# Seven mixer projections and half of an embedding gate as joint blocks with seven-product pairs in an fp32 encoder layer

## The chip, the core and the metric

One core of one Trainium2 chip. The time is device microseconds of one execution. Every matmul is 128x128 by 128x512, in fp32r. To reach fp32 accuracy, each fp32 product is made as three matmuls: every operand is split into a rounded part (hi) and a remainder (lo), and lo·hi, hi·hi and hi·lo are summed in PSUM.

## The reference

256 tokens, 2048 features, weights in fp32 that are each used once. Cut to what matters here:

```
h = h + 1/2 * SwiGLU_1(RMSNorm(h))                # 2048 -> 5632 -> 2048
u = RMSNorm(h); z = u @ W_in                      # columns: NA q|k|v (1024 each), q-latent 512,
                                                  # kv-latent 512, rope key 64, gate_A 2048, gate_B 2048
A  = NeighbourhoodAttention2D(q, k, v) @ W_branch_A      # 8 heads, with a table of biases
Bm = MLA(q-latent, kv-latent, rope key) @ W_branch_B     # 8 heads, through W_uq and W_ukv
h = h + (sigmoid(gate_A) * A + sigmoid(gate_B) * Bm) @ W_out
h = h + 1/2 * SwiGLU_2(RMSNorm(h))
h = h + sigmoid(RMSNorm(h) @ W_pl_gate) * (p @ W_pl)     # per-layer embedding
out = RMSNorm(h)
```

## The kernel before, in words

**Stream of granules.** The main loop (line 1160 on) walks a list of granules, each a step. A granule has a conversion and its matmuls. The conversion (`conv`) starts the load of raw weights on SyncE's queue into one of three raw tiles R, and then `split` (L89) makes hi on ScalarE (the cast L90) and lo on VectorE (the subtraction L91) into tiles W0 to W5. `convert()` runs ahead in the list for as long as W tags are free; a tag comes back when its granule's matmuls are done. All engines keep the order in which the program issues: in each step first the conversions that have tags, then the granule's matmuls (`triple`, L95 to L97), then the step's tasks. `at(d, fn)` puts a task d steps later. Tasks are evacuations' second halves, transposes, attention and sums of squares.

**Plain units.** `unit` computes 256 tokens by 512 columns; with K row tiles of 128 that is 6K matmuls (96 for K = 16), in granules of two row tiles (12 matmuls, one W tag out of W0 to W3). Its sums stand in two of PSUM banks 0 to 3; side work (`bank()`) takes banks 4 to 7. The stationary operand is x transposed, split into hi and lo, the moving one the weights.

**Joint blocks.** `Block` computes two such 512-column products at once over pairs of row tiles, so each pair is a 2x2 by 2x2 block product. A plain pair (`Plain`) needs 8 products of three matmuls, 24. Pairs 2, 4 and 6 (`SEVEN`) use seven products of sums of the operands, 21 matmuls, issued as `SevenA` (9) and `SevenB` (12). They need sums of weights on VectorE (L258 to L261) and a "form" of x with eight tiles (`sums` on VectorE, L358, and a second split). A pair takes two W tags out of six, so two pairs lie converted ahead of the one in use. The products accumulate in all eight banks: plain pairs use banks 4, 5, 7 and 3; SevenA begins bank 0; SevenB begins banks 6, 2 and 1 in this order among its products. At the block's end VectorE combines the eight sums in eight additions, `early` (L192 to L195) and `late` (L201 to L204), and `done` takes the four results. While a block runs, side work has only those of banks 0 to 2 that its products have not begun.

**Forms.** `make_form` transposes four 128x128 tiles of h (or of a product) into one bank, scales it on ScalarE by the norm's gain, and takes lo on VectorE. For a seven-product pair it first writes a scratch tile Z on ScalarE, makes sums there on VectorE, and one step later splits Z into hi and lo.

**Where joint blocks are used.** In both SwiGLUs: 11 chunks of gate and up (the first chunk of the layer excepted), and the down products, in three parts, two blocks each. All of the mixer and the embedding is plain units: three latents and the rope key, W_ukv and W_uq, NA q, k, v, gate_B, then for each of four column groups gate_A, branch A and branch B, then W_out. MLA attention runs as tasks beside the NA projections (a head pair every five granules), NA attention beside the gate_B units. When the last down block of a SwiGLU is done, `added` adds its results to h on VectorE (L549) and `new_xT` transposes, scales and splits the new x (L332, L336, L344) for the plain units behind it; sums of squares follow four to six steps later. The table of NA biases is loaded by 16 DMAs on POOL's queue (L822) while the NA projections run, and POOL masks it with eight `affine_select`s (L827, L829). `na_qk_evac` scales a result on VectorE (L840) and transposes it one step later (L847).

## Time and profile before

| | |
|---|---|
| median of 3 runs | 2152.14 us (2151.56 to 2153.6) |
| the profiled execution | 2156.39 us, its span 2154.7 us |
| mean granted TensorE clock in it | 0.997 |
| largest groups | L91 on VectorE 1066.4 us in 697 operations, L90 on ScalarE 911.5 us in 697 |
| loads of weights | 408.46 MB on SyncE's queue, 57.2% of the DMA engines' span |

The lines of the trace are in us from the span's start. A timeline row has start, length, engine, line, operation, what it writes and reads, a count, and in brackets the idle time before it and what ended that. A windows row has the stretch, its length, and for each of PE, PEld, DVE, ACT and POOL the busy us and instructions, then the mean granted clock, the DMA share and GB/s. Matmul records are longer than their spacing, since matmuls overlap.

### The profile page before, as it was taken

To read this page: it belongs to the slowest core of one execution; us is meant where nothing else is said; L and a number is where in the kernel's file an instruction comes from. 1 tells how busy PE (TensorE), PEld (TensorE's weight loads), DVE (VectorE), ACT (ScalarE), POOL (GpSimd) and SP (SyncE) were. 2 spreads that over 40 slices of the span, in tenths; PEclk is the share of its full clock that TensorE was granted. 3 is DMA by queue.
4 is the path that set the end of the run, shared out by engine and by line. 5 is a ranking of instruction groups with operands and counts; after the bars stand their busy time and mean duration, and the time that the engine had idled before them with its cause. 6 is when DMAs were issued, how large, how long until landed. Compare 5 with 4: busy or idle time off the path is not lost.

```text
span 2154.7 us, 25398 instructions
## 1 busy us (share of the span) xinstructions
PE 2138.3 (99%) x9693; PEld 1774.8 (82%) x9693; DVE 1716.2 (80%) x1856; ACT 1137.0 (53%) x1172; POOL 62.9 (3%) x73
## 2 busy tenths in 40 slices
PE   9999999999999999999999999999999999999997
PEld 8888888888888888878888888888888888888886
DVE  6899889998999855555655556999989998899975
ACT  7455555554555554435544445555545555555553
POOL 0000100000000000230000000000000000000000
PEclk9999999999999999999999999999999999999999
DMA  7555766667565554565455556466676657765653
GB/s 262 189 195 196 238 196 205 202 212 236 196 205 185 169 194 138 158 192 176 144 189 195 187 185 207 164 197 202 218 228 205 205 191 215 220 209 184 220 197 127
DMA packets 218026, 421.99 MB, mean 196 GB/s; under 512 B 13576, under 2 KB 14160, under 8 KB 217776
## 3 DMA queue, kind: packets, MB, share of 16 engines
q1 hardware_dynamic: 212048, 408.46, 57.2%
q0 software_dynamic: 5824, 11.89, 3.2%
q8 instruction: 76, 1.25, 0.2%
q14 instruction: 46, 0.38, 0.0%
q10 hardware_dynamic: 32, 0.01, 0.0%
HBM read 409.83 MB, written 2.10 MB: 191 GB/s over the span
## 4 chain that ended last, share of the span: by engine, by line
PE 97%; DVE 1%; DMA 1%; ACT 0%; issue 0%; POOL 0%; DVEq 0%; ACTq 0%; POOLq 0%
PE B L97 31%; PE B L95 31%; PE B L96 31%; PE B L368 1%; DMA R<-in_w_in_dram 1%; PE B L776 1%; PE B L344 0%; DVE W L91 0%; PE B L762 0%; PE B L800 0%; PE B L883 0%; PE B L801 0%; ACT W L90 0%; PE B L847 0%; PE B L1121 0%
## 5 line engine op out<-in xcount | busy, mean ns | idle before, releaser
L91 DVE TENSOR_TENSOR W<-R,W 128x1024 fp32r<-128x1024 f32 (+2 forms) x697 | 1066.4, 1548 | 318.4 <-ACT W L90 315.9
L90 ACT CAST W<-R 128x1024 fp32r<-128x1024 f32 (+2 forms) x697 | 911.5, 1311 | 722.6 <-DVE R L258 290.3
L95 PE MATMUL B<-W,X 128*128 128x512 f32 x2113 | 832.8, 394 | 0.0
L97 PE MATMUL B<-W,X 128*128 128x512 f32 x2113 | 823.9, 390 | 0.5 <-DVE W L91 0.5
L96 PE MATMUL B<-W,X 128*128 128x512 f32 x2113 | 823.1, 390 | 0.0
L97 PEld LDWEIGHTS B<-W,X 128*128 128x128 f32 x2113 | 397.1, 188 | 84.7 <-DVE W L91 1.1
L96 PEld LDWEIGHTS B<-W,X 128*128 128x128 f32 x2113 | 397.4, 188 | 80.8
L95 PEld LDWEIGHTS B<-W,X 128*128 128x128 f32 x2113 | 397.4, 188 | 80.7
L95 PE MATMUL B<-W,H 128*128 128x512 f32 x800 | 312.6, 391 | 0.2 <-DVE X L336 0.2
L97 PE MATMUL B<-W,H 128*128 128x512 f32 x800 | 311.6, 390 | 0.3 <-DVE W L91 0.3
L96 PE MATMUL B<-W,H 128*128 128x512 f32 x800 | 311.3, 389 | 0.0
L97 PEld LDWEIGHTS B<-W,H 128*128 128x128 f32 x800 | 150.2, 188 | 32.2 <-DVE W L91 1.1
L95 PEld LDWEIGHTS B<-W,H 128*128 128x128 f32 x800 | 150.2, 188 | 31.5 <-issue 0.8
L96 PEld LDWEIGHTS B<-W,H 128*128 128x128 f32 x800 | 150.2, 188 | 30.8
L258 DVE TENSOR_TENSOR R<-R 128x1024 f32<-128x1024 f32 x95 | 116.4, 1225 | 3.3
L261 DVE TENSOR_TENSOR R<-R 128x512 f32<-128x512 f32 x95 | 65.8, 693 | 3.2
L260 DVE TENSOR_TENSOR R<-R 128x512 f32<-128x512 f32 x95 | 65.7, 692 | 3.3
L386 ACT CAST H<-B 128x512 fp32r<-128x512 f32 x28 | 15.9, 588 | 90.5 <-PE B L368 90.5
L551 POOL DMA_DIRECT2D h<-t x16 | 14.1, 1018 | 1409.3 <-DVE t L201 1189.6
L538 ACT ACTIVATE s<-t,sm 128x512 f32<-128x512 f32 x42 | 28.1, 717 | 31.9 <-DVE t L201 31.9
L539 DVE SCALAR_TENSOR_TENSOR pt<-pt,sm,s 128x512 f32<-128x512 f32 x42 | 29.5, 744 | 0.0
L332 ACT ACTIVATE X<-B,gT 128x256 fp32r<-128x256 f32 x40 | 15.7, 478 | 25.3 <-PE B L344 25.3
(207 smaller groups left out, 1024.5 us busy)
## 6 DMA issues: line engine op xcount, KB each, us to landing
R<-in_ffn_w_down_dram SPq DMA_DIRECT2D x176, 512.0 KB, 5.2
R<-in_ffn_w_gate_dram SPq DMA_DIRECT2D x170, 512.0 KB, 3.7
R<-in_ffn_w_up_dram SPq DMA_DIRECT2D x168, 512.0 KB, 4.7
R<-in_w_in_dram SPq DMA_DIRECT2D x64, 1024.0 KB, 5.2
R<-in_w_out_dram SPq DMA_DIRECT2D x16, 1024.0 KB, 5.0
R<-in_w_pl_gate_dram SPq DMA_DIRECT2D x16, 1024.0 KB, 5.1
R<-in_w_branch_a_dram SPq DMA_DIRECT2D x8, 1024.0 KB, 4.9
R<-in_w_branch_b_dram SPq DMA_DIRECT2D x8, 1024.0 KB, 4.9
```

The lines of the kernel that those rows point to most:

```text
L90: S.copy(hi, r)
L91: V.tensor_tensor(out=lo, in0=r, in1=hi.bitcast(F32), op=ALU.subtract)
L95: PE.matmul(o, xl, hi, start=start, stop=False)
L96: PE.matmul(o, xh, hi, start=False, stop=False)
L97: PE.matmul(o, xh, lo, start=False, stop=stop)
L258: V.tensor_tensor(out=raw[:, 0:4:3, :], in0=raw[:, 0:3:2, :], in1=raw[:, 3:4, :].to_broadcast([P, 2, 512]), op=ALU.add)
L260: V.tensor_tensor(out=raw[:, 2, :], in0=raw[:, 0, :], in1=raw[:, 2, :], op=ALU.add)
L261: V.tensor_tensor(out=raw[:, 1, :], in0=raw[:, 2, :], in1=raw[:, 1, :], op=ALU.add)
L368: PE.transpose(ps[:, j * P:j * P + P], src(t, 2 * i + k), ident)
L538: S.activation(s[t], g, AF.Silu, scale=r[:, t:t + 1])
L539: V.scalar_tensor_tensor(out=u, in0=u, scalar=rh[:, t:t + 1], in1=s[t], op0=ALU.mult, op1=ALU.mult)
L776: PE.matmul(b[:, j * T:j * T + T], vsl(heads[j], kt), pts[j][:, kt, :], start=(kt == 0), stop=(kt == 1))
```

## The change

Joint blocks take the place of plain units for: kv-latent with q-latent, NA v, the second half of gate_B, gate_A (two blocks), W_out (two blocks), and the first half of the embedding gate. The order of units changes: latents, NA q (first half), rope key, W_ukv, W_uq, rest of q, k, v; branch B, gate_B, gate_A, branch A, W_out. x is held in forms throughout (`first_tile` reads plain tiles from them), so `new_xT` goes and `added` calls `new_forms` after both blocks: forms of the first 512 columns one step, of the second two steps later, sums of squares at steps five and six. All seven-product forms of h share the scratch tag Z; a pending split is flushed before Z is taken again. `bank()` inside a block gives out banks 0, 1, 2, 1, 2 in this order from its start. MLA and NA attention run a head pair every four granules, beside plain units only, and hold W4 and W5 meanwhile (`hold`, `loose`). The bias load moves to one step after the v block, and VectorE masks it eight steps later by adding a window tile. NA's output is kept in fp32 and split once at the end. The core of the diff:

```diff
     def bank():
+        if seven_on[0]:
+            turn["block"] += 1
+            return psum_tile((0, 1, 2, 1, 2)[turn["block"] - 1])
         turn["side"] += 1
-        if seven_on[0]:
-            return psum_tile((1, 2, 0)[turn["side"] % 3])
         return psum_tile(4 + turn["side"] % 4)
...
+    pending = []
+
+    def flush():
+        while pending:
+            pending.pop()()
+
-    def make_form(where, i, j, src, gc=None):
+    def make_form(where, i, j, src, gc=None, full=False, scratch="Z"):
...
-        z = piece("Z", [P, 8, P])
+        flush()
+        z = piece(scratch, [P, 8, P])
+        c = 0 if full else 1
         scaled(z[:, 0:4, :].rearrange("p a b -> p (a b)"), ps, gc)
         sums(z[:, 0:4, :], z[:, 4:8, :])
-        at(1, lambda: split(f[:, 0, 1:8], f[:, 1, 1:8], z[:, 1:8, :]))
+        pending.append(lambda: split(f[:, 0, c:8], f[:, 1, c:8], z[:, c:8, :]))
+        at(1, flush)
         return f
...
+    def added(n, nxt, full=True):
+
+        def done(c11, c12, c21, c22):
+            for k, t, o in ((n, 0, c11), (n, 1, c21), (n + 1, 0, c12), (n + 1, 1, c22)):
+                hs = h[:, t, k * 512:k * 512 + 512]
+                if nxt:
+                    V.tensor_tensor(out=hs, in0=hs, in1=o, op=ALU.add)
+                else:
+                    G.dma_start(hs, o, accum_op=ALU.add)
+            if nxt:
+                for k in range(2):
+                    at(1 + k, lambda k=k: new_forms(n + k, nxt, full))
+                    next_stat(nxt, n + k, 5 + k)
+        return done
...
-                if n == 0:
-                    at(1, lambda: new_xT(0, nxt))
-                    at(1, lambda: new_xT(1, nxt, (0,)))
-                    at(2, lambda: new_xT(1, nxt, (1,)))
-                    next_stat(nxt, 0, 5)
-                    next_stat(nxt, 1, 6)
-                else:
-                    at(2, lambda: new_xT(2, nxt))
-                    at(3, lambda: new_xT(3, nxt))
-                    next_stat(nxt, 2, 4)
-                    next_stat(nxt, 3, 5)
...
+        def latents(c11, c12, c21, c22):
...
+            for d, (which, place, z) in enumerate((("kva", "H0", (c11, c21)), ("qa", "H2", (c12, c22)))):
+                for t in range(2):
+                    V.tensor_scalar(out=z[t], in0=z[t], scalar1=r[:, t:t + 1], scalar2=None, op0=ALU.mult)
+                at(1 + 2 * d, lambda which=which, place=place, z=z: tr(which, place, z))
...
+            def masked():
+                for t in range(2):
+                    q = M["bias"][t].rearrange("p a i c -> p (a i) c")
+                    V.tensor_tensor(out=q, in0=q, in1=window[:, None, :].to_broadcast([P, 32, 64]), op=ALU.add)
+            at(9, masked)
+            at(1, bias)
...
+        joint(wi, 3584, 3072, x, latents)
+        plain(0, na_qk_evac("nq", 0, "H1"))
+        unit(rows(wi, 4096, 64), 16, 64, narrow_x, kr_evac)
         for u in range(4):
             unit(rows(w_ukv[0], u * 512), 4, 512, lop("kva"), ukv_evac(u))
         for u in range(3):
             unit(rows(w_uq[0], u * 512), 4, 512, lop("qa"), uq_evac(u))
+        plain(512, na_qk_evac("nq", 1, "H1"))
         for u in range(2):
+            plain(1024 + u * 512, na_qk_evac("nk", u, "H3"))
+        joint(wi, 2048, 2560, x, values)
         for n in range(4):
+            unit(rows(w_branch_b[0], n * 512), 8, 512, oop("ob"), yb_evac(n))
+        for n in range(2):
+            plain(6208 + n * 512, gb_evac(n))
+        joint(wi, 6208 + 1024, 6208 + 1536, x, gb_done(2))
+        for n in (0, 2):
+            joint(wi, 4160 + n * 512, 4160 + n * 512 + 512, x, ga_done(n))
         for n in range(4):
             unit(rows(w_branch_a[0], n * 512), 8, 512, oop("oa"), ya_evac(n))
+        for n in (0, 2):
+            joint(w_out[0], n * 512, n * 512 + 512, form_of(mixed), added(n, "ffn2", False))
...
+        wg, wp = w_pl_gate[0], w_pl[0]
+        Block([rows(wg, 0), rows(wg, 512)], form_of(forms), 8, gates)
+        unit(rows(wp, 0), 2, 512, pop, pl_evac(0))
+        unit(rows(wp, 512), 2, 512, pop, pl_evac(1))
+        unit(rows(wg, 1024), 16, 512, None, gate_evac(2), xtile=first_tile)
...
-    tasks.setdefault(first_pl + 4, []).append(E["ptr"])
+    tasks.setdefault(first_pl + 1, []).append(lambda: at(1, E["ptr"]))
```

`E["ptr"]` transposes the embedding's input p into one bank and splits it (ScalarE, then VectorE).

## The prediction

> **What bounds the kernel now.** I read the page first: busy shares, then the chain that ended last.

> ```profile
> span 2154.7 us, 25398 instructions
> PE 2138.3 (99%) x9693; PEld 1774.8 (82%) x9693; DVE 1716.2 (80%) x1856; ACT 1137.0 (53%) x1172; POOL 62.9 (3%) x73
> ...
> PE 97%; DVE 1%; DMA 1%; ACT 0%; issue 0%; POOL 0%; DVEq 0%; ACTq 0%; POOLq 0%
> ```

> The chain is TensorE almost from end to end, so the time is the number of matmuls times their spacing, plus the places where TensorE waits. The windows view gives the spacing, for a joint gate-and-up block and the joint down block behind it:

> ```profile
> 428.99:471.36 42.37, 42.37 (x193) 35.17 (x192) 39.78 (x40) 24.05 (x22) 0.00 (x0) 1.00 0.60 199
> 471.36:512.84 41.48, 41.48 (x185) 34.35 (x184) 36.13 (x32) 20.84 (x17) 3.48 (x4) 1.00 0.75 230
> ```

> The second has no transposes. By the listing a joint block of eight pairs is 5 x 24 + 3 x 21 = 183 matmuls: 41.48 / 183 = 0.2267 us each, with no wait. The first has eight transposes more: 0.89 us, 0.11 each. But VectorE is busy 39.78 of 42.37 us there: joint blocks run at TensorE's pace with little to spare.

> The timelines of one block start show how little. It is the last down block of the first SwiGLU, which already hands on to the mixer with additions into h and transposed forms. TensorE:

> ```profile
> 677.60 0.39 PE L95 MATMUL B<-W,H 128*128 128x512 f32 x1
> ...
> 689.59 0.39 PE L97 MATMUL B<-W,H 128*128 128x512 f32 x1
> 689.83 0.60 PE L344 MATMUL B<-ident,h 128*128 128x128 f32 x4
> ...
> 692.81 0.39 PE L97 MATMUL B<-W,H 128*128 128x512 f32 x1
> 693.44 0.47 PE L95 MATMUL B<-W,H 128*128 128x512 f32 x1 [0.25 <-DVE X L336]
> ...
> 695.60 0.39 PE L95 MATMUL B<-W,H 128*128 128x512 f32 x1
> ...
> 696.06 0.39 PE L97 MATMUL B<-W,H 128*128 128x512 f32 x1
> ```

> VectorE, then ScalarE:

> ```profile
> 678.22 0.68 DVE L204 TENSOR_TENSOR pt<-B,pt 128x512 f32<-128x512 f32 x1
> 678.82 2.28 DVE L91 TENSOR_TENSOR W<-R,W 128x2048 fp32r<-128x2048 f32 x1
> 681.01 1.29 DVE L549 TENSOR_TENSOR h<-h,t 128x512 f32<-128x512 f32 x2
> ...
> 683.42 1.75 DVE L91 TENSOR_TENSOR W<-R,W 128x1536 fp32r<-128x1536 f32 x1
> 685.21 1.23 DVE L258 TENSOR_TENSOR R<-R 128x1024 f32<-128x1024 f32 x1
> ...
> 687.80 2.44 DVE L336 SCALAR_TENSOR_TENSOR X<-B,gT,X 128x256 fp32r<-128x256 f32 x6
> 690.16 2.35 DVE L91 TENSOR_TENSOR W<-R,W 128x1024 fp32r<-128x1024 f32 x2
> 692.42 0.87 DVE L336 SCALAR_TENSOR_TENSOR X<-B,gT,X 128x256 fp32r<-128x256 f32 x2
> 693.21 3.95 DVE L91 TENSOR_TENSOR W<-R,W 128x2048 fp32r<-128x2048 f32 x2
> ```

> ```profile
> 690.46 0.84 ACT L332 ACTIVATE X<-B,gT 128x256 fp32r<-128x256 f32 x2 [1.49 <-PE B L344]
> ...
> 699.91 1.05 ACT L90 CAST W<-R 128x1024 fp32r<-128x1024 f32 x1 [0.32 <-DVE R L261]
> ...
> 702.11 1.89 ACT L90 CAST W<-R 128x2048 fp32r<-128x2048 f32 x1
> ```

> Three things are to be seen. VectorE runs without a gap from 678.82. Pair 3 (the plain pair behind the first seven-product pair) has its remainder ready at 693.21 + 2.2 = 695.4; TensorE needs it at that pair's third matmul, 696.06, or at 695.65 without the 0.41 us lost at 693.44. So 0.25 us is the whole margin. And that 0.41 us is a PSUM bank: the transposes after pair 1 used a bank that the seven-product pair's second half fills, and VectorE emptied it late.

> **What it removes.** Eight joint blocks (seven in the mixer, one in the embedding) take the place of sixteen plain projections: 2 x 96 - 183 = 9 matmuls each, 72 x 0.2267 = 16.3 us. The transposes stay as many. Second, the mask work and the bias load. Now:

> ```profile
> 902.84 8.27 POOL L822 DMA_DIRECT2D H<-in_na_rpb_dram  x12 [196.09 <-PE B L776]
> ```

> ```profile
> 923.98 1.99 ACT L90 CAST W<-R 128x1024 fp32r<-128x1024 f32 x2 [6.28 <-DMA R<-in_w_in_dram]
> ```

> ```profile
> 926.84 1.40 DVE L840 TENSOR_SCALAR t<-B,sm 128x512 f32<-128x512 f32 x2
> ```

> ```profile
> 924.37 0.39 PE L97 MATMUL B<-W,X 128*128 128x512 f32 x1
> 927.63 0.47 PE L847 MATMUL B<-ident,t 128*128 128x128 f32 x1 [2.87 <-DVE t L840]
> 928.29 1.76 PE L847 MATMUL B<-ident,t 128*128 128x128 f32 x7 [0.18 <-DVE t L840]
> 929.70 0.78 PE L95 MATMUL B<-W,X 128*128 128x512 f32 x1
> ...
> 933.69 0.40 PE L95 MATMUL B<-W,X 128*128 128x512 f32 x1
> ```

> ```profile
> 925.00:930.00 5.00, 2.18 (x9) 1.89 (x10) 4.48 (x4) 1.56 (x3) 4.87 (x3) 0.68 0.45 165
> ```

> The bias load delays a weight load; ScalarE waits for it, VectorE behind ScalarE; the evacuation L840 stands in VectorE's queue behind conversions that TensorE does not need yet, and the transposes of that result wait for L840. Eight transposes and nine matmuls after 924.37 would have put the next matmul at 924.37 + 0.23 + 0.87 + 2.04 = 927.5; it stands at 933.69: 6.2 us lost. Of these 3.6 are waits (3.0 and 0.5) and 2.6 the halved clock after them (matmuls 0.43 us apart until 933.69). After the change the load runs beside the branch-b projections, whose evacuations nothing on TensorE needs soon; ten granules, 27 us, pass before the first score matmul. ScalarE waited 6.3 us for its weights, less than the 10.9 us that four converted granules last TensorE. I take the whole 6.2 us as gained; the bounds are 0 and 6.2. POOL's masking becomes two VectorE additions of 128x2048, 2.3 us each by the row at 678.82, hidden in plain units, where VectorE has half its time:

> ```profile
> 935.00:1000.00 65.00, 65.00 (x289) 53.80 (x288) 29.41 (x24) 29.95 (x32) 0.00 (x0) 1.00 0.58 182
> ```

> **What it adds.** Additions into h and forms move to block starts, into the queues above. Seven-product forms cost these (a gate-and-up block's):

> ```profile
> 445.03 1.01 DVE L358 TENSOR_TENSOR Z<-Z 128x128 f32<-128x128 f32 x4
> ...
> 448.24 1.09 DVE L91 TENSOR_TENSOR H<-Z,H 128x896 fp32r<-128x896 f32 x1
> ```

> First FFN2 block. From 678.82 on VectorE's queue now holds: pair 1's remainder 2.19, additions 2.41, pair 2 (1.79, and 2.59 of weight sums up to 687.80), form 5 0.79, sums for form 4 1.01, second half 2.26, form 7 0.79, split of form 4 1.09: 14.9. Form 6 needs the same scratch tile Z as form 4, so ScalarE may write it only now: 0.84. Pair 3's cast is queued behind it: 1.89; then its remainder 2.28. With handovers 20.1: 698.9 against a need at 695.65 (sixteen transposes there too). TensorE waits 3.3 us.

> Pair 5 waits as well. In the trace its cast follows h's squares at 702.11, its remainder at

> ```profile
> 704.03 3.43 DVE L91 TENSOR_TENSOR W<-R,W 128x2048 fp32r<-128x2048 f32 x2 [1.80 <-ACT W L90]
> ```

> ends near 706.2, and TensorE's third matmul already waits 0.12 us:

> ```profile
> 706.38 0.50 PE L97 MATMUL B<-W,H 128*128 128x512 f32 x1
> ```

> The split of form 6 (or 2) now stands ahead of this chain: 1.09 more, and about 0.5 because pair 3 left no margin: 1.7 us. So 5.0 for this block.

> Latents block: the same, but the down block ahead of it ends VectorE-bound (its own pair 5), so the last evacuation trails TensorE by 2.19 + 8 x 0.60 + handovers - 22 x 0.2267 = 2.1 us, where the rows show 678.82 - 677.60 = 1.2. That adds 0.9: 5.9. At its end the latents are scaled and transposed one granule later: 1.2 + two conversions 2.35 + two scalings, by the nearest row of the groups view

> ```profile
> L1074 DVE TENSOR_SCALAR H<-H,sm 128x512 f32<-128x512 f32 x4 | 1.8, 483 | 0.1
> ```

> 0.97 = 4.5 us, where the granule is 12 x 0.2267 = 2.7: 1.9 with the release.

> Last down blocks of both SwiGLUs and second W_out block: only one seven-product form, so no scratch conflict: 0.3 at pair 3, 1.7 at pair 5. W_out 2.0; a down block 1.5 over today's 0.5, two of them 3.0.

> Embedding's block: as the latents', and the transposes of p are a fifth use of the three side banks, bank 2, directly ahead of the second half, whose second product fills bank 2. Their remainder (0.7, with handovers 0.9) stands on VectorE behind pair 3's, which is 4.2 us late as in the latents block; TensorE stops there with eleven matmuls (2.5) still to do before pair 3's third: 4.2 + 0.9 + 2.5 - 0.44 (the transposes) = 7.1 us. That is one wait of over 5 us, longer than the 3.0 us at 924.6 that halved the clock, so I add its 2.6.

> Edits at nothing: attention's head pairs every four granules instead of five. The offsets inside a pair stay, and VectorE's idle half of the plain units hides the denser softmax; without that cover a pair would cost up to a granule, 2.7 us, eight pairs 22. The v, gate_B and gate_A blocks start and end without additions and transposes; with them each would cost what W_out's does, 2.0.

> Sum: 3.0 + 5.9 + 1.9 + 2.0 + 5.0 + 7.1 + 2.6 = 27.5 lost, 16.3 + 6.2 = 22.5 gained: +5.0. The waits are bounded by 0 (all absorbed) and by 27.5 + 1.8 (below); I take the sum, because its chain is the traced one with known operations put in. The profiled execution took 2156.39 us (span 2154.7), 4.25 over the median 2152.14; it becomes 2161.4, and the median 2157.1, say 2157.

> The waits of 3.3 and 4.2 us at pair 3 fall into two parts of half that, with two matmuls between. By the row at 927.63, where two waits with one transpose between halved the clock, they would cost 2.6 each, of which pair 5's 1.7 is swallowed: +0.9 each, +1.8 in all. [...] No run here shows such a split wait.

> **Rivals.** Faster: the block starts absorb the new work. Deciding point: pair 3's remainder in the first FFN2 block must land before its third matmul. For it: the chain above is added up from single rows, and VectorE does idle (1.80 us at 704.03). Against it: the margin today is 0.25 us and the additions are 3 us. With none of the waits: 2152.1 - 22.5 = 2129.6; with a third of them, without the clock, 2138.

> Same: the waits come, the clock stays whole: 2154.5.

> Slower still: the bias load, now where the lead is just rebuilt after a joint block, stalls TensorE as before: 2157.1 + 6.2 = 2163.3. Against it: no transposes stand behind those evacuations.

> Oscillation: each of the ten or so waits costs a half-clock stretch of 2.6: about 2180. Against it: the 0.41 us wait left matmuls 0.23 apart. [...]

> Not as described: matmul counts other than 72 fewer: 2 in 100.

> **Chances.** Main case 0.42, clock whole 0.20, absorbed 0.20, bias 0.13, oscillation 0.03, other 0.02. No change is within 0.2%, 2147.8 to 2156.4, about what a measurement can tell. The main case (2151 to 2162) straddles its upper edge: 0.25 slower, 0.17 same. The second gives 0.16 same, 0.04 slower; the absorbed 0.19 faster; bias and oscillation are slower. Sum: faster 0.20, same 0.35, slower 0.45. The range reaches down into the absorbed case and up past the bias case: 2140 to 2165.

> **What would show it.** TensorE records 72 matmuls fewer. The first FFN2 block's pair 3 starts 3 us late behind ScalarE's cast, that behind the form in Z; the embedding block stops over 5 us at the seventh product's bank, with the granted clock at a half after it; the branch-b stretch shows no wait. I am wrong if VectorE idles between the first additions and pair 3's remainder there.

## The result and the profile after

The changed kernel takes 2184.15 us (median of 4 runs, 2180.34 to 2185.14), the kernel before 2152.22 beside it: ratio 1.0144, interval 1.0127 to 1.0162. It is slower by 32 us, where 2157 was forecast with a range up to 2165.

The profiled execution of after took 2180.34 us. Its page, from the span, the busy shares and the chain that ended last:

```profile
span 2178.6 us, 25574 instructions
PE 2132.2 (98%) x9621; PEld 1762.7 (81%) x9621; DVE 1857.8 (85%) x2005; ACT 1175.9 (54%) x1178; POOL 46.5 (2%) x70
...
PE 91%; DVE 4%; ACT 2%; issue 2%; DMA 1%; DVEq 0%; ACTq 0%; POOL 0%; POOLq 0%
```

TensorE records are 9621 against 9693: the 72 fewer matmuls are there, 16.3 us less work for TensorE. But TensorE has 91% of the chain instead of 97%; VectorE and ScalarE come in with 6%, and VectorE has 142 us more to do. The waits view of after (who waited, who ended it: us in total, times, longest) says where:

```profile
PE B L97 <- DVE W L91: 12.2, 10, 1.6
PE B L95 <- DVE H L337: 7.6, 1, 7.6
PE B L95 <- ACT W L90: 5.9, 2, 3.0
PE B L95 <- DVE t L201: 2.4, 3, 1.1
PE B L769 <- DVE P L756: 2.1, 2, 1.2
PE B L353 <- DVE t L623: 2.0, 1, 2.0
PE B L1152 <- POOL ident L293: 1.4, 1, 1.4
PE B L95 <- ACT Z L393: 0.6, 2, 0.4
...
```

The row of L1152 is the start of the program, as before. All others shown are new or grown. To set them against the forecast I took each stretch of TensorE's timeline, summed the distances of neighbouring starts, and took off the median distance of each form of matmul. What is left is lost time, waits and halved clock together: 52.0 us after, 11.8 before. By stretch, after less before:

| Stretch | forecast | measured |
|---|---|---|
| 72 matmuls | -16.3 | -16.3 |
| bias stall in the NA projections | -6.2 | -5.8 |
| last down block of SwiGLU 1, up to the next block's start | +1.5 | +2.6 |
| latents block | +5.9 | +9.3 |
| its end | +1.9 | +2.4 |
| NA attention | 0 | +2.5 |
| first branch-A unit | 0 | +1.7 |
| second W_out block | +2.0 | +2.1 |
| first FFN2 block | +5.0 | +10.8 |
| last down block of SwiGLU 2 | +1.5 | +2.3 |
| embedding block and what follows | +9.7 | +11.9 |
| elsewhere | 0 | +0.4 |
| sum | +5.0 | +23.9 |

The sum is the difference of the spans, 2178.6 - 2154.7. Signs and places of the forecast hold; the sizes at the block starts do not. The windows view of after for the NA projections with the v block, where the kernel before stalled, and for the three branch-B units beside which the biases are loaded now (POOL is busy 10.94 us there):

```profile
840.55:977.25 136.70, 136.70 (x649) 114.96 (x647) 87.58 (x118) 66.58 (x96) 0.00 (x0) 1.00 0.48 157
977.25:1011.71 34.46, 34.46 (x153) 28.55 (x152) 21.28 (x20) 15.44 (x21) 10.94 (x16) 1.00 0.85 227
```

TensorE is busy throughout at the full clock in both: the stall is gone from there.

Now the latents block around pair 3, TensorE, then ScalarE, then VectorE:

```profile
735.98 0.50 PE L95 MATMUL B<-W,X 128*128 128x512 f32 x1 [3.02 <-ACT W L90]
...
738.30 0.79 PE L97 MATMUL B<-W,X 128*128 128x512 f32 x1 [1.59 <-DVE W L91]
738.90 0.63 PE L95 MATMUL B<-W,X 128*128 128x512 f32 x1
739.32 0.63 PE L96 MATMUL B<-W,X 128*128 128x512 f32 x1
```

```profile
731.10 0.84 ACT L393 ACTIVATE Z<-B,gT 128x256 f32<-128x256 f32 x2 [2.33 <-DVE X L91]
733.08 1.04 ACT L90 CAST X<-Z 128x1024 fp32r<-128x1024 f32 x1 [1.14 <-DVE Z L362]
734.03 3.27 ACT L90 CAST W<-R 128x2048 fp32r<-128x2048 f32 x2
```

```profile
731.97 1.02 DVE L362 TENSOR_TENSOR Z<-Z 128x128 f32<-128x128 f32 x4 [0.97 <-ACT Z L393]
734.16 1.23 DVE L91 TENSOR_TENSOR X<-Z,X 128x1024 fp32r<-128x1024 f32 x1 [1.17 <-ACT X L90]
735.96 3.96 DVE L91 TENSOR_TENSOR W<-R,W 128x2048 fp32r<-128x2048 f32 x2 [0.57 <-ACT W L90]
```

Read ScalarE downwards: the scratch tile Z for form 6, then the cast of form 6 from Z into X, and only then pair 3's weights W. The forecast had the cast X<-Z behind pair 3's. VectorE follows in the same order, and stands idle 0.97, 1.17 and 0.57 us between: the two engines hand each other one small step at a time, with everything else queued behind. The forecast had named VectorE idling at this point of the first FFN2 block as what would make it wrong; there the same gaps are 0.97, 1.06 and 0.71 us. TensorE's last two rows are 0.42 us apart instead of 0.23: the clock was halved. The windows view shows when:

```profile
733.22:736.64 3.42, 0.66 (x2) 0.30 (x2) 1.91 (x2) 3.42 (x3) 0.00 (x0) 1.00 0.09 28
736.64:740.05 3.41, 1.81 (x5) 1.46 (x5) 3.38 (x3) 0.66 (x1) 0.00 (x0) 0.50 0.19 26
740.05:743.46 3.41, 3.41 (x9) 2.64 (x9) 3.34 (x4) 1.84 (x2) 0.00 (x0) 0.50 0.75 282
```

The first FFN2 block does the same at 1366.38 (2.91 and 1.59 us), with the clock at a half from 1368.10 to 1374.93. In the embedding block the bank wait comes first, as forecast; TensorE, then VectorE:

```profile
2073.90 0.40 PE L97 MATMUL B<-W,X 128*128 128x512 f32 x1
2081.91 0.79 PE L95 MATMUL B<-W,X 128*128 128x512 f32 x1 [7.62 <-DVE H L337]
```

```profile
2077.16 1.23 DVE L91 TENSOR_TENSOR X<-Z,X 128x1024 fp32r<-128x1024 f32 x1 [1.17 <-ACT X L90]
2078.96 2.29 DVE L91 TENSOR_TENSOR W<-R,W 128x2048 fp32r<-128x2048 f32 x1 [0.57 <-ACT W L90]
2081.17 0.68 DVE L337 TENSOR_TENSOR H<-B,H 128x512 fp32r<-128x512 f32 x1
```

Form 6's split, pair 3's remainder, p's remainder: the third empties the bank.

### The profile page after: what moved, and what is told of

It reads as the page before. It is cut to its first block, busy times and chain, and to the rows that moved or that the text cites. A ratio compares the mean times of both kernels' runs of the same rounds, so it can differ in the third digit from the quotient of the medians.

```text
span 2178.6 us, 25574 instructions
## 1 busy us (share of the span) xinstructions
PE 2132.2 (98%) x9621; PEld 1762.7 (81%) x9621; DVE 1857.8 (85%) x2005; ACT 1175.9 (54%) x1178; POOL 46.5 (2%) x70
## 3 DMA queue, kind: packets, MB, share of 16 engines
q8 instruction: 75, 1.23, 0.2%
## 4 chain that ended last, share of the span: by engine, by line
PE 91%; DVE 4%; ACT 2%; issue 2%; DMA 1%; DVEq 0%; ACTq 0%; POOL 0%; POOLq 0%
PE B L97 29%; PE B L95 29%; PE B L96 29%; DVE W L91 2%; PE B L372 2%; ACT W L90 1%; DMA R<-in_w_branch_b_dram 1%; PE B L783 1%; PE B L769 0%; PE B L811 0%; PE B L810 0%; DVE X L91 0%; ACT sq L468 0%; PE B L894 0%; ACT Z L393 0%
## 5 line engine op out<-in xcount | busy, mean ns | idle before, releaser
L90 ACT CAST W<-R 128x1024 fp32r<-128x1024 f32 (+2 forms) x681 | 936.8, 1382 | 674.3 <-DVE R L259 365.3
L91 DVE TENSOR_TENSOR W<-R,W 128x1024 fp32r<-128x1024 f32 (+2 forms) x681 | 1094.5, 1629 | 211.9 <-ACT W L90 210.3
L95 PE MATMUL B<-W,X 128*128 128x512 f32 x2019 | 796.8, 395 | 16.9 <-DVE H L337 7.6
L97 PE MATMUL B<-W,X 128*128 128x512 f32 x2019 | 789.8, 391 | 6.5 <-DVE W L91 6.5
L96 PE MATMUL B<-W,X 128*128 128x512 f32 x2019 | 788.2, 390 | 0.0
L95 PEld LDWEIGHTS B<-W,X 128*128 128x128 f32 x2019 | 380.8, 189 | 98.7 <-DVE H L337 8.0
L97 PEld LDWEIGHTS B<-W,X 128*128 128x128 f32 x2019 | 380.6, 189 | 88.9 <-DVE W L91 9.1
L96 PEld LDWEIGHTS B<-W,X 128*128 128x128 f32 x2019 | 381.0, 189 | 77.5
L97 PE MATMUL B<-W,H 128*128 128x512 f32 x934 | 364.5, 390 | 6.0 <-DVE W L91 5.7
L95 PE MATMUL B<-W,H 128*128 128x512 f32 x934 | 366.2, 392 | 0.0
L96 PE MATMUL B<-W,H 128*128 128x512 f32 x934 | 363.5, 389 | 0.0
L97 PEld LDWEIGHTS B<-W,H 128*128 128x128 f32 x934 | 175.3, 188 | 45.4 <-DVE W L91 9.0
L96 PEld LDWEIGHTS B<-W,H 128*128 128x128 f32 x934 | 175.4, 188 | 36.0
L95 PEld LDWEIGHTS B<-W,H 128*128 128x128 f32 x934 | 175.4, 188 | 35.7
L259 DVE TENSOR_TENSOR R<-R 128x1024 f32<-128x1024 f32 x119 | 145.8, 1225 | 4.1
L262 DVE TENSOR_TENSOR R<-R 128x512 f32<-128x512 f32 x119 | 82.4, 693 | 4.0
L261 DVE TENSOR_TENSOR R<-R 128x512 f32<-128x512 f32 x119 | 82.4, 692 | 4.1
L193 DVE TENSOR_TENSOR t<-B,pt 128x512 f32<-128x512 f32 x41 | 28.4, 692 | 1.4
```

What stands on the lines that cost most here:

```text
L90: S.copy(hi, r)
L91: V.tensor_tensor(out=lo, in0=r, in1=hi.bitcast(F32), op=ALU.subtract)
L95: PE.matmul(o, xl, hi, start=start, stop=False)
L96: PE.matmul(o, xh, hi, start=False, stop=False)
L97: PE.matmul(o, xh, lo, start=False, stop=stop)
L193: V.tensor_tensor(out=self.v, in0=q[7], in1=self.w, op=ALU.add)
```

## The experiments

**Theory.** The lost time is a matter of queue positions behind additions into h. In the trace of after all 2005 operations of VectorE and all 1092 casts, copies and activations of ScalarE start in the order in which the program issues them, so conversions that TensorE needs soon stand behind forms, splits and squares that it needs later. **Rivals:** ScalarE and VectorE simply have too much to do at a block start, so that whatever leaves one place waits at the next; or a joint block costs something wherever it stands.

**The early split.** The task that form 4 leaves for the next step, `flush`, empties the whole list of pending splits, and the next step has just put form 6 on it. This edit makes the task split its own form only (`x5_own_split`):

```diff
-        pending.append(lambda: split(f[:, 0, c:8], f[:, 1, c:8], z[:, c:8, :]))
-        at(1, flush)
+        part = lambda: split(f[:, 0, c:8], f[:, 1, c:8], z[:, c:8, :])
+        pending.append(part)
+        at(1, lambda: part in pending and (pending.remove(part), part()))
```

> The changed kernel with one edit: the task that a seven-product form registers for one granule later now splits only that form, not whatever is pending. So in the three blocks that take fresh forms, form 6's split (1.04 us on ScalarE, 1.23 on VectorE) is issued behind pair 3's cast and remainder instead of ahead of them. Theory (the early split is part of the pair-3 waits of 3.2 + 1.8 us, and their length is what halves the clock): each pair-3 wait shrinks by about 1.1 us in the latents block and the first SwiGLU-2 block, a wait of up to 1.7 us for form 6's place in the queue shows at pair 5 instead, and if the wait falls under what halves the clock the two stretches of 2.1 and 2.6 us go: 2175 to 2182 us. Rival (the split's place does not matter, the chain form 4, scratch Z, form 6, cast alone sets the wait): 2183 to 2185, both half-clock stretches stay.

Measured: 2176.32 us, ratio 1.0104 (1.0090 to 1.0118), 7.8 us less than the changed kernel by the medians, 4.1 between the two profiled executions. ScalarE, VectorE and TensorE in its latents block:

```profile
731.36 0.84 ACT L393 ACTIVATE Z<-B,gT 128x256 f32<-128x256 f32 x2 [2.32 <-DVE X L91]
732.09 1.90 ACT L90 CAST W<-R 128x2048 fp32r<-128x2048 f32 x1
733.88 1.05 ACT L90 CAST X<-Z 128x1024 fp32r<-128x1024 f32 x1
```

```profile
734.02 2.29 DVE L91 TENSOR_TENSOR W<-R,W 128x2048 fp32r<-128x2048 f32 x1 [0.77 <-ACT W L90]
736.23 1.22 DVE L91 TENSOR_TENSOR X<-Z,X 128x1024 fp32r<-128x1024 f32 x1
```

```profile
734.04 0.50 PE L95 MATMUL B<-W,X 128*128 128x512 f32 x1 [0.82 <-ACT W L90]
736.37 0.50 PE L97 MATMUL B<-W,X 128*128 128x512 f32 x1 [1.59 <-DVE W L91]
```

Cast and remainder of pair 3 now come first, and TensorE's wait for the cast falls from 3.02 to 0.82 us. That is twice the 1.1 expected: the cast had waited for form 6's sums on VectorE too (the idle 1.14 above). No wait over 0.1 us shows at pair 5, so the 1.7 us that the expectation put there did not come; pairs 6 and 7 wait 0.28 and 1.07 us instead, where in the changed kernel pair 7 alone waits 0.88. The halved clock did not go: behind 0.82 and 1.59 us close together it is 0.50 from 737.02 on, and in the first FFN2 block from 1365.07, so that part of the theory fell.

**Two scratch tiles.** Forms of the last 512 columns use H3 in place of Z, so form 6 needn't wait for form 4's split (`x1_scratch`):

```diff
-            forms[i] = make_form(XPLACE, i, i, h_tile, gcol[gname] + 2 * i, full)
+            forms[i] = make_form(XPLACE, i, i, h_tile, gcol[gname] + 2 * i, full, "H3" if n == 3 else "Z")
```

> The changed kernel, with one edit: the seven-product form of the last 512 columns takes another scratch tile (H3) than the one before it (Z). Queue theory (TensorE waits at block starts because the added forms and additions stand ahead of pair 3's conversion in the queues of ScalarE and VectorE): ScalarE's wait for Z, 6.9 us in three places in the trace of the changed kernel, goes, so pair 3 comes some 1.8 us earlier in the latents block and the first FFN2 block; 3.6 us faster, and up to 5 more if the halved clock after these waits goes too; 2175 to 2181. Density theory (joint blocks behind one another leave VectorE no room, wherever its work stands): no change, 2184.

Measured: 2176.89 us, ratio 1.0107 (1.0092 to 1.0122). The wait for Z is gone and the two waits at pair 3 are down to 2.6 and 2.4 us for the cast:

```profile
PE B L95 <- ACT W L90: 5.0, 2, 2.6
```

**p's transposes moved.** They leave the embedding block's start for its end, and take bank 0 there (`x2_ptr_end`):

```diff
-            return psum_tile((0, 1, 2, 1, 2)[turn["block"] - 1])
+            return psum_tile((0, 1, 2, 1, 0)[turn["block"] - 1])
...
-    tasks.setdefault(first_pl + 1, []).append(lambda: at(1, E["ptr"]))
+    tasks.setdefault(first_pl + 9, []).append(lambda: at(1, E["ptr"]))
```

> The changed kernel, with the transposes of p moved to the end of the embedding's joint block, into bank 0. Queue theory: the 7.8 us wait for the bank goes, but pair 3 of that block then waits for its own conversion as in the latents block (5 us, with a halved clock behind it), and the first p product waits 1 to 2 us for p: 0 to 4 us faster, 2180 to 2184. If the bank is the cause by itself: 8 to 11 us faster, 2173 to 2176.

Measured: 2179.53 us, ratio 1.0121 (1.0104 to 1.0138). In its waits view the 7.6 us for L337 became 1.4, but ScalarE's cast of W is waited for three times instead of twice:

```profile
PE B L95 <- ACT W L90: 9.0, 3, 3.0
...
PE B L95 <- DVE H L337: 1.4, 1, 1.4
```

So the bank alone was not the price. Behind it stood the same late pair 3 as in the other two blocks.

**Squares one granule later** (`x3_squares_later`):

```diff
-                    next_stat(nxt, n + k, 5 + k)
+                    next_stat(nxt, n + k, 6 + k)
```

> The changed kernel, with the sums of squares of h one step later (steps 6 and 7 instead of 5 and 6), so behind pair 5's cast on ScalarE. Queue theory: the waits at the last pair of both final down blocks (1.6 us each), the bank waits of 1.2 us at the next blocks' starts that follow from them, and the 1.5 us at pair 5 of the second W_out block go: 5 to 8 us faster, 2176 to 2179. Density theory: no change, 2184.

Measured: 2179.18 us, ratio 1.0117 (1.0101 to 1.0132). TensorE's waits at pair 5 of the last down blocks fall from 1.46 and 1.45 us to 0.25 and 0.21, W_out's 1.32 goes, and the 0.9 to 1.1 us at pair 7 of three other blocks fall to about 0.3. Waits for remainders in all, 12.2 us before this edit:

```profile
PE B L97 <- DVE W L91: 5.9, 9, 1.6
```

The time fell by 5.0 us. Part of the gain is taken back: in this trace NA attention waits 3.7 us instead of 2.1, and the clock is halved in five places instead of three (its mean 0.991 against 0.993).

**All of it together.** The own split, the second scratch tile, p's move and the later squares, and two more: NA pairs every five granules as in the kernel before, and W4 and W5 opened to the branch-A weights (`x6_mended`):

```diff
-                run(pair, d0 + 4 * pair)
+                run(pair, d0 + 5 * pair)
...
-            at(d0 + 17, end)
+            at(d0 + 20, end)
...
-            unit(rows(w_branch_a[0], n * 512), 8, 512, oop("oa"), ya_evac(n))
+            unit(rows(w_branch_a[0], n * 512), 8, 512, oop("oa"), ya_evac(n), pool=6)
```

> The changed kernel with all eight joint blocks kept and six edits to the order of the work around them: the own split, a second scratch tile for the last 512 columns' forms, squares of h one granule later, p's transposes at the embedding block's end through bank 0, neighbourhood pairs every five granules, and branch-a weights allowed into all six conversion tiles. Theory (the waits are queue positions at block starts and each edit removes its own): the single gains of the runs so far add up, about 2 + 7 + 5 + 5 from the first four, 2.5 from the pair spacing and 1.6 from the tiles, and 2161 us comes out, 2158 to 2166; the bank waits of 1.25 us at the next block's start stay. Rival (ScalarE and VectorE have no slack at a block start, so whatever is taken out of one place waits at the next): 2168 to 2178.

Measured: 2159.51 us, ratio 1.0032 (1.0022 to 1.0043). With all eight joint blocks and all matmuls kept, 24.6 of the 32 us are back by moving work and opening three tiles and a bank to it, and no clock is halved before the kernel's end (its mean 0.998). Most of the waits did not pass on to the next place (the rival's 2168 to 2178), so the first rival falls. What is left is many smaller waits: 2.0 us each at the ends of the latents and the embedding block, 1.5 in NA attention, 1.4 for p's remainder, 1.3 to 1.4 at pair 3 of three blocks, and 1.1 us each for a bank at the start of the block behind a last down block (L202 here). It is still slower than the kernel before.

**No joint block straight behind an addition.** Seven of the eight new joint blocks stay, and none of them meets fresh forms; the first FFN2 block, which the kernel before has too, still does. The first NA q unit goes ahead of the latents block, a gate unit ahead of the embedding's block, W_out's second half becomes plain, and forms and p's transposes behind an addition come later (`x4_behind_plain`; the core):

```diff
-        joint(wi, 3584, 3072, x, latents)
         plain(0, na_qk_evac("nq", 0, "H1"))
+        joint(wi, 3584, 3072, x, latents)
         unit(rows(wi, 4096, 64), 16, 64, narrow_x, kr_evac)
...
-        for n in (0, 2):
-            joint(w_out[0], n * 512, n * 512 + 512, form_of(mixed), added(n, "ffn2", False))
+        joint(w_out[0], 0, 512, form_of(mixed), added(0, "ffn2", False, 2))
+        for n in (2, 3):
+            unit(rows(w_out[0], n * 512), 16, 512, None, wout_evac(n), xtile=mixed_tile)
...
+        unit(rows(wg, 1024), 16, 512, None, gate_evac(2), xtile=first_tile)
         Block([rows(wg, 0), rows(wg, 512)], form_of(forms), 8, gates)
```

> Seven of the eight joint blocks stay, but none of them takes in h's additions and forms except the first FFN2 block, which takes them in without a joint block's end ahead of it: the first NA q unit goes ahead of the latents block, the third embedding gate unit ahead of the embedding's block, and the second half of W_out is two plain units; p is transposed beside the plain unit. Queue theory: 63 matmuls fewer than before (14.3 us), the bias wait gone (6.2 us), left over the waits in the two final down blocks (3), NA attention (2.4), branch A (1.6) and some in FFN2's first block (1 to 4): 9 to 13 us faster than before, 2139 to 2143. Density theory: the seven joint blocks still cost more than they save, slower than before, over 2152.

Measured: 2158.13 us, ratio 1.0017 (1.0008 to 1.0027): 26 us faster than the changed kernel with one joint block fewer, but some 17 short of what I expected, and by its number in the rival's range (over 2152). The trace says where, and it is not inside the moved blocks. The first FFN2 block still met forms 4 to 7 made behind the last W_out unit, and lost 7.4 us, with the clock at a half from 1356.40 to 1363.23:

```profile
1355.01 0.50 PE L95 MATMUL B<-W,X 128*128 128x512 f32 x1 [2.47 <-ACT W L90]
1357.34 0.80 PE L97 MATMUL B<-W,X 128*128 128x512 f32 x1 [1.60 <-DVE W L91]
```

The units behind the latents and the embedding block lose another 3.1 and 4.4 us, which I had not counted: they wait for operands made from the block's results and for VectorE's evacuations. So the ends of these two blocks do cost something here.

**Only the inner joint blocks**: v, half of gate_B, gate_A; latents, W_out and embedding plain as in the kernel before (`x7_inner`; the core):

```diff
-        joint(wi, 3584, 3072, x, latents)
-        plain(0, na_qk_evac("nq", 0, "H1"))
+        plain(3584, lat_evac("kva", "H0"))
         unit(rows(wi, 4096, 64), 16, 64, narrow_x, kr_evac)
+        plain(3072, lat_evac("qa", "H2"))
...
-        for n in (0, 2):
-            joint(w_out[0], n * 512, n * 512 + 512, form_of(mixed), added(n, "ffn2", False))
+        for n in range(4):
+            unit(rows(w_out[0], n * 512), 16, 512, mop, wout_evac(n))
...
-        Block([rows(wg, 0), rows(wg, 512)], form_of(forms), 8, gates)
```

> Only the joint blocks inside the mixer that take neither fresh additions nor fresh forms are kept (v, half of gate_B, two for gate_A); the latents, W_out and the embedding gate go back to plain units, with the layout and the attention's spacing of the changed kernel. 36 matmuls fewer than before instead of 72. Theory (the lost time stands at the starts of the blocks that follow an addition into h): 8.2 us of matmuls and 6.2 us of bias wait gained against the kernel before, 2.5 lost in neighbourhood attention, 1.6 at the first branch-a unit, about 3 at the last down blocks' pair 5: 2143 to 2148 us, faster than before. Rival (joint blocks cost at their ends or starve the plain units whatever they follow): 2151 or more.

Measured: 2155.55 us, ratio 1.0010 (1.0001 to 1.0018), not the 2143 to 2148 expected. The number is in the rival's range (2151 or more), but the joint blocks kept were not to blame: inside them TensorE loses nothing, and the waits in NA attention and at the first branch-A unit behind them were in the sum. What was not in it are 5.8 us, by the two traces, that the plain units behind the last down blocks lose against the kernel before, with a halved clock from 2043.68; TensorE:

```profile
2042.69 1.09 PE L372 MATMUL B<-ident,h 128*128 128x128 f32 x8 [2.77 <-DVE h L535]
```

The transposes of columns 1024 to 2047 are issued one granule behind the block and wait for the additions. The kernel before made them two granules behind when plain units followed; I had left the changed kernel's step.

**Three edits to that**: the own split, NA pairs every five granules, six tiles for branch A (`x8_inner_mended`):

```diff
-        at(1, flush)
+        at(1, lambda: part in pending and (pending.remove(part), part()))
...
-                run(pair, d0 + 4 * pair)
+                run(pair, d0 + 5 * pair)
...
-            unit(rows(w_branch_a[0], n * 512), 8, 512, oop("oa"), ya_evac(n))
+            unit(rows(w_branch_a[0], n * 512), 8, 512, oop("oa"), ya_evac(n), pool=6)
```

> The kernel of the run with only the inner joint blocks, and three edits: the own split, neighbourhood pairs every five granules, branch-a weights allowed into all six conversion tiles. Theory: the two waits of 1.3 and 1.1 us for the softmax scaling and the one of 1.6 at the first branch-a unit go, nothing else moves: 3 to 4.5 us less than that run, 2139 to 2144. Rival (these waits pass to the next consumer): within 1 us of it.

Measured: 2151.92 us, ratio 0.9991 (0.9982 to 1.0000), 3.6 less, as expected against that run; the 2139 to 2144 rested on that run's own forecast. The wait at the first branch-A unit and one of NA's two are gone. The other is 1.25 us, and some of the gain is chance: the transposes still wait 2.79 us, but this time no halved clock follows, which is worth 1.6 us. VectorE, then TensorE:

```profile
2036.54 2.35 DVE L91 TENSOR_TENSOR W<-R,W 128x1024 fp32r<-128x1024 f32 x2
2038.81 1.29 DVE L537 TENSOR_TENSOR h<-h,t 128x512 f32<-128x512 f32 x2
2040.01 1.29 DVE L537 TENSOR_TENSOR h<-h,pt 128x512 f32<-128x512 f32 x2
```

```profile
2040.15 1.09 PE L373 MATMUL B<-ident,h 128*128 128x128 f32 x8 [2.79 <-DVE h L537]
```

**Forms one granule later where plain units follow the last down block, and squares and NA one granule later** (`x9_inner_late`):

```diff
-                    at(1 + k, lambda k=k: new_forms(n + k, nxt, full))
-                    next_stat(nxt, n + k, 5 + k)
+                    d = 1 if n == 0 else 2
+                    at(d + k, lambda k=k: new_forms(n + k, nxt, full))
+                    next_stat(nxt, n + k, (6 if n == 0 else 5) + k)
...
-            na_attention(10)
+            na_attention(11)
...
-            at(9, masked)
+            at(10, masked)
```

> The kernel of the run with the inner joint blocks and three edits, with three more: behind a last down block the forms of the new columns are made two and three granules later instead of one and two (as in the kernel before), the squares of the first half of h one granule later, and neighbourhood attention starts one granule later with its mask. Theory (even a plain unit waits if the transposes of freshly added columns are issued before VectorE has added them): the 0.7 us at 715 and the 2.9 us at 2037 with the halved clock behind it (2.2) go, the two 1.6 us waits at pair 5 shrink to 0.4, most of the 1.4 us in neighbourhood attention goes: 2152 less 3.6, 2.2, 2.4 and 1 gives 2143, 2141 to 2147 us, faster than before. Rival (the additions only wait elsewhere): 2149 to 2152.

Measured: 2144.15 us, ratio 0.9955 (0.9941 to 0.9968), faster than both kernels, and where the theory had it. The same transposes:

```profile
2036.66 1.09 PE L373 MATMUL B<-ident,h 128*128 128x128 f32 x8 [0.41 <-DVE h L537]
```

**Half of W_out joint again** (`x10_half_wout`; the core):

```diff
-        for n in range(4):
-            unit(rows(w_out[0], n * 512), 16, 512, mop, wout_evac(n))
+        joint(w_out[0], 0, 512, form_of(mixed), added(0, "ffn2", False))
+        for n in (2, 3):
+            unit(rows(w_out[0], n * 512), 16, 512, None, wout_evac(n), xtile=mixed_tile)
```

> The kernel of the run with the forms two and three granules later, and the first half of W_out as a joint block once more, its second half as two plain units behind it: nine matmuls fewer, 2.0 us, with fresh forms met by plain units alone. Theory: 2.0 us less than that run, 2139 to 2145. Rival (the seven-product forms of the mixed columns, made in the branch-a units, or the additions behind the joint block cost their own wait): equal or up to 3 us more than that run.

Measured: 2143.75 us, ratio 0.9955 (0.9942 to 0.9967). Nine matmuls fewer, and 1.6 of their 2.0 us lost again behind the block:

```profile
1285.90 0.50 PE L97 MATMUL B<-W,H 128*128 128x512 f32 x1 [1.47 <-DVE W L91]
```

**Six tiles for W_out's plain units** (`x11_six_tiles`), then **their transposes one granule later too** (`x12_later_forms`):

```diff
-            unit(rows(w_out[0], n * 512), 16, 512, None, wout_evac(n), xtile=mixed_tile)
+            unit(rows(w_out[0], n * 512), 16, 512, None, wout_evac(n), xtile=mixed_tile, pool=6)
```

```diff
-        joint(w_out[0], 0, 512, form_of(mixed), added(0, "ffn2", False))
+        joint(w_out[0], 0, 512, form_of(mixed), added(0, "ffn2", False, True))
```

> The kernel of the run with half of W_out joint, and one edit: its two plain units may convert into all six conversion tiles instead of the first four. Theory (a joint block's last pair hands back W4 and W5, which a plain unit could not use, so its first conversion was issued only behind the block's last evacuations on VectorE, 1.63 us of wait at 1284; the same happened at the first branch-a unit of the changed kernel): that wait goes and nothing takes its place, 1.6 us less than that run, 2142 us, 2140.5 to 2143.2. Rival (the tile is not what the conversion waits for, or the wait passes to the next granule): 2143.5 to 2145.

> The kernel of the run with six tiles for W_out's plain units, and one edit: behind W_out's joint half the transposes of the freshly added columns are issued two and three granules later instead of one and two, as already behind the last down blocks. Theory (transposes issued one granule behind a joint block reach TensorE before VectorE has done the additions; in the six-tile run this showed as 2.2 us at 1286 with a halved clock of 1.2 behind it, once the tile wait that had hidden it was gone): 3.5 us less than that run, 2143 us, 2140.5 to 2144.5. Rival (the lead is used up there, and whatever comes first behind the block waits): 2145.5 to 2147.5.

Measured: 2146.54 us, ratio 0.9969 (0.9957 to 0.9981), then 2143.50, ratio 0.9950 (0.9936 to 0.9963). With the tiles alone the conversion was in time, and TensorE ran into the next thing sooner, the transposes, at the price of a halved clock:

```profile
1288.30 1.72 PE L373 MATMUL B<-ident,h 128*128 128x128 f32 x8 [2.02 <-DVE h L537]
```

Here the rival's mechanism was right (the wait passes on, at more than it had priced), until the second edit took that wait away as well; nothing is lost in W_out then. But both runs have a new wait of 1.5 us in the first embedding unit, right behind the last down block, that neither the run with the forms later nor that with half of W_out joint has. VectorE, then TensorE, in the last run:

```profile
2028.37 0.69 DVE L205 TENSOR_TENSOR pt<-B,pt 128x512 f32<-128x512 f32 x1 [0.21 <-PE B L97]
2028.98 2.35 DVE L91 TENSOR_TENSOR W<-R,W 128x1024 fp32r<-128x1024 f32 x2
```

```profile
2030.25 0.50 PE L97 MATMUL B<-W,X 128*128 128x512 f32 x1 [1.46 <-DVE W L91]
```

The remainder that TensorE needs (L91) stands behind the last evacuation of the block (L205). By the listing this is the same tile wait one block further on. Giving W4 and W5 to W_out's units changes the order in which the tags come back: in the last down block the first half of pair 4 now holds W4 and W5, and pair 5 holds W3 and W0. The embedding's unit may not take W4 and W5, so its first conversion is issued one granule later, behind those evacuations. In the two runs without the wait pair 5 holds W4 and W5. No run opened the tiles to that unit too. The versions at 2144.15, 2143.75 and 2143.50 can't be told apart.

## Why the prediction was wrong

**The step that failed** is the walk of the queues behind the last additions. It put pair 3's cast right behind the form in Z ("Pair 3's cast is queued behind it: 1.89") and form 6's split ahead of pair 5 only. I had read the task that form 4 leaves as having nothing left to do. In the listing it runs in the very step that puts form 6 on the list, and takes it. So the split stood ahead of pair 3, which costs 2.2 us there (3.02 against 0.82, shown by the one edit), and the 1.7 forecast at pair 5 did not come.

Nor was the walk right in the order that it assumed, which is that of the own-split run. The two waits at pair 3 are 2.4 us there (0.82 and 1.59) in the latents and the FFN2 block alike, against 4.2 and 3.3 forecast, nothing waits at pair 5, and the embedding's bank costs 5.41 against 7.1. That the changed kernel's 7.62 came close to 7.1 is luck. What the walk had at nothing is pair 7: 0.88 to 1.05 us in three blocks, for a remainder behind the squares of h, as the run with the squares later shows (0.32 to 0.34).

**The clock.** By the row at 927.63 the split waits at pair 3 would halve the clock. I took the sum with the clock whole there, which no run had shown, and kept the row's +1.8 as a bound. The row was right, and by more than the +0.9 taken for each: by the spacing of the matmuls after the waits the halved stretches cost 2.1 us in the latents block and 2.6 in the first FFN2 block. The embedding's, forecast at 2.6, cost 1.1, since most of it passed while TensorE stood anyway.

**Costs put at nothing.** Of the 5.8 us gained 2.5 come back in NA attention. About half of that is a price that the bias load moved rather than lost: it delays weights again, now those of branch B, and behind their late conversions the mask stands on VectorE until 1008.2, just when the scores are due (no run moves the mask alone). ScalarE's and VectorE's rows in after, then TensorE's:

```profile
999.57 1.05 ACT L90 CAST W<-R 128x1024 fp32r<-128x1024 f32 x1 [4.75 <-DMA R<-in_w_branch_b_dram]
```

```profile
1003.72 4.49 DVE L874 TENSOR_TENSOR W<-W,window 128x2048 f32<-128x2048 f32 x2
```

```profile
1015.89 0.98 PE L769 MATMUL B<-ident,P 128*128 128x128 f32 x7 [1.17 <-DVE P L756]
```

The other half, 0.94 us at 1063.07, is the head pairs every four granules, put at nothing too: with pairs every five granules it is gone, and the first wait stays (1.25 us in the inner kernel with three edits). With the start one granule later as well that one went (the run with the forms later). The first branch-A unit: gate_A's last block hands back W4 and W5, which a plain unit could not take, so its first conversion was issued behind the block's last evacuations; opening the tiles took that wait away in two kernels. And a block's start waits 1.1 us behind both last down blocks for L201, which empties bank 4, the one that the next block's first product fills; the forecast's walk stopped short of the next block.

**From the profiled run to the median.** I took off 4.25 us, as the kernel before's profiled run stood above its median. After's profiled run was the fastest of its four: the median lies 3.8 above it. The terms missed by 18.9 us (23.9 against 5.0), this step by 8.1; together that is the miss of 27.

**What held.** The matmuls saved, the stall gone from the NA projections, the W_out block at 2.0, and the places and releasers of the waits in the latents, FFN2 and embedding blocks. The oscillation rival gave 2180 but not by its mechanism: three halved stretches, 5.8 us in all, not one for each wait.

## What to carry to other kernels

When work is queued behind an addition that the next block's operands depend on, write out the issue order of every engine from the listing, deferred tasks included, and ask of each item whether TensorE needs it before the one it delays; here moving items, with three tiles and a bank opened to them, took no matmul away and gave back 24.6 of 32 us. A saving in matmuls is worth what is left after the start of the block: 9 matmuls are 2.0 us, and one split in the wrong place cost 2.2. Put the fused form where no fresh operand meets it first, and give the freshly added columns two granules before they are transposed.

## What the runs showed of the hardware

```profile
1361.65:1365.07 3.42, 1.70 (x5) 0.78 (x5) 2.43 (x5) 3.42 (x4) 0.00 (x0) 1.00 0.55 213
```

```profile
1007.51:1010.92 3.41, 1.84 (x12) 1.25 (x11) 3.37 (x7) 3.14 (x7) 0.00 (x0) 1.00 0.80 284
```

In the four stretches inside before and after, the clock stayed at a half behind a window in which the profile has TensorE idle for 0.61 us or more (2.80 busy of 3.41 at 1368.10 in after) and was whole again behind one in which it is idle for 0.42 or less (2.99 busy at 2081.49).

In the own-split kernel's latents block waits of 0.82 and 1.59 us with two matmuls between them were followed by the halved clock (0.50 from 737.02 on). A wait of one length was cheap or dear by where it fell. The transposes of the inner kernels show it: 2.77 us, most of it in one window (PE busy 0.99 us of 2040.26 to 2043.68), halved the clock; 2.79 us in the next kernel, cut by a window's edge at 2038.93 (busy 1.85 and 2.19), did not.
